# Row sums on one core: the seven rows that were loaded ahead of the whole groups go to the end

## The chip, the core and the metric

The kernel runs on one core of a Trainium2 chip. The metric is the time of one execution in microseconds (us). Before the change it is 161.35 us, the median of three runs (161.17, 161.35, 161.35).

The core's engines that matter here are SyncE (SP), which issues the loads and the last store; VectorE (DVE) and ScalarE (ACT), which add up rows; and 16 DMA engines, which move the data from the device memory (HBM) into the on-chip memory with its 128 partitions.

## The reference

The input `x` has 32 x 512 x 1024 float32 numbers, 67.1 MB. The output is the sum over the last axis, 32 x 512 numbers:

```python
return np.sum(x, axis=-1).astype(np.float32)
```

Each number is read once and added once, and the output is 64 KB.

## The kernel before

The 16,384 rows of 1024 numbers are spread over the 128 partitions, 128 rows to each. A group is 16 rows per partition (`BIG`): 16 x 1024 x 4 bytes are 64 KB per partition and 8.39 MB over all of them. There are eight groups. One, here called A, is the first 2048 rows of `x`, where a partition's 16 rows lie right behind those of the partition before (`x_a`). The other seven come from the rest (`x_b`), in which each partition has 112 rows in a row; they are called G (its rows 0 to 15) and B1 to B6 (rows 16 to 111). `rows_from` (L131) takes j below 112 as a place in `x_b`, and j from 112 on as one in `x_a`.

Each group needs an input buffer `t`, and there are three of them (L141), taken in turn. The order of the work is written out by hand; every engine follows the program's order, and the framework puts in the waits that the data needs. The steps before the change:

1. SP issues the first seven rows of G (L214, called F here) into the first buffer. A routine moves this very first load to the program's entry (L10). Its reduction on DVE is remembered as `first` (L215).
2. `wholes` (L216) lists A and then B1 to B6. The loop issues one load of 8.39 MB for each. A goes to the buffer `second`, of which DVE first fills four rows with zeros (L213); A's load therefore waits for that fill. B1's load (k == 1) is held until `first` is done (L223). From then on a load waits for the reduction that empties its buffer.
3. A and B1 to B5 are each summed by one DVE instruction of 128 x 16384 numbers (`vec`, L151). B6, the last, is summed row by row: nine rows on DVE, by an instruction that adds the two halves of a row and accumulates (`halves`, L164), and seven on ACT (`act`, L177).
4. The other nine rows of G follow in a fresh buffer (L227 to L237): a load of six rows (four on DVE, two on ACT), one of two rows (one and one), and the last row in two pieces of 560 and 464 numbers. DVE adds up the first piece into a cell behind the second, and the second with that cell.
5. Three stores put out the sums. Two, on ACT's queue, wait until the load of two rows has landed (L239, L240). The last, with the sums of G, goes from SP after the last DVE instruction (L243).

Of the kernel before, what the change touches and what calls it, by code (L numbers as in the profile page):

```python
# [100 lines left out]
@with_exitstack  # L101
def kernel(
    ctx: ExitStack,
    tc: tile.TileContext,
    x: bass.AP,
    out: bass.AP,
):
    nc = tc.nc
    nc.at_finalize(issue_first_load_at_entry)
    nc.at_finalize(order_waits)  # L110
    nc.at_finalize(wait_for_the_store_at_the_clear)
    fp32 = mybir.dt.float32
    P = 128
    batch, seq, dim = x.shape
    rows = batch * seq
    J = rows // P
    BIG = 16

    LONG = J - BIG
    rows_in = x.flatten_outer_dims()
    rows_out = out.rearrange("b s -> (b s)")
    x_a = rows_in[: P * BIG].rearrange("(p j) d -> p j d", p=P)
    x_b = rows_in[P * BIG :].rearrange("(p j) d -> p j d", p=P)
    out_a = rows_out[: P * BIG].rearrange("(p j) -> p j", p=P)
    out_b = rows_out[P * BIG :].rearrange("(p j) -> p j", p=P)


    def rows_from(j, n):  # L131
        return x_b[:, j : j + n, :] if j < LONG else x_a[:, j - LONG : j - LONG + n, :]

    last = 0
    FIRST = 7
    pieces = (560, 464)
    LINE = 64

    with (
        tc.tile_pool(name="small", bufs=1) as smallpool,  # L140
        tc.tile_pool(name="in", bufs=3) as inpool,  # L141
        tc.tile_pool(name="unread", bufs=4, space=bass.MemoryType.PSUM) as upool,
        tc.tile_pool(name="stage", bufs=1) as stpool,
        tc.manual_schedule(),
    ):


        seed = smallpool.tile([P, LINE // 2], fp32)
        sums = stpool.tile([P, J], fp32)

        def vec(dst, src):  # L151
            return nc.vector.tensor_reduce(  # L152
                out=dst, in_=src, axis=mybir.AxisListType.X, op=mybir.AluOpType.add
            )

        def hold(inst, until, reason):
            tc.add_manual_dep(
                inst.ins,
                until.ins.name,
                mybir.DependencyInfo(mybir.DependencyClass.Sync, mybir.DependencyReason.DATA),  # L160
                reason=reason,
            )

        def halves(dst, src):  # L164
            n = src.shape[-1] // 2
            return nc.vector.tensor_tensor_reduce(  # L166
                out=src[:, :n],
                in0=src[:, :n],
                in1=src[:, n:],
                scale=1.0,  # L170
                scalar=0.0,
                op0=mybir.AluOpType.add,
                op1=mybir.AluOpType.add,
                accum_out=dst,
            )

        def act(dst, src, n):  # L177
            unread = upool.tile([P, dim], fp32)
            nc.scalar.activation(  # L179
                out=unread[:, :n],  # L180
                in_=src,
                func=mybir.ActivationFunctionType.Copy,
                accum_out=dst,
            )

        sums_of = []

        def rows(t, a, n, j, n_act, pairs=False):
            nv = n - n_act
            block = t[:, a * dim : (a + n) * dim].rearrange("p (n d) -> p n d", d=dim)  # L190
            load = nc.sync.dma_start(out=block, in_=rows_from(j, n))  # L191
            if pairs:
                for q in range(nv):
                    sums_of.append(halves(sums[:, j + q : j + q + 1], block[:, q, :]))
            else:
                sums_of.append(vec(sums[:, j : j + nv], block[:, :nv, :]))
            for q in range(nv, n):
                act(sums[:, j + q : j + q + 1], block[:, q, :], dim)
            return load

        def store(eng, dst, j0, j1):
            return eng.dma_start(out=dst, in_=sums[:, j0:j1])

        nc.vector.memset(seed[:, :1], 0.0)  # L204
        unread = upool.tile([P, dim], fp32)
        ready = nc.scalar.activation(  # L206
            out=unread[:, :1], in_=seed[:, :1], func=mybir.ActivationFunctionType.Copy
        )

        j = last  # L210
        t = inpool.tile([P, BIG * dim + LINE], fp32)
        second = inpool.tile([P, BIG * dim + LINE], fp32, name="t")
        nc.vector.memset(second[:, : 4 * dim], 0.0)  # L213
        rows(t, 0, FIRST, j, 0)  # L214
        first = sums_of[-1]  # L215
        wholes = [LONG, *range(BIG, LONG, BIG)]  # L216
        for k, at in enumerate(wholes):
            t = second if k == 0 else inpool.tile([P, BIG * dim + LINE], fp32)
            if k < len(wholes) - 1:
                load = rows(t, 0, BIG, at, 0)  # L220
            else:
                rows(t, 0, BIG, at, 7, pairs=True)
            if k == 1:  # L223
                hold(load, first, "no descriptors of later loads while the first ones start")

        t = inpool.tile([P, BIG * dim + LINE], fp32)
        rows(t, FIRST, 6, j + FIRST, 2, pairs=True)  # L227
        two = rows(t, FIRST + 6, 2, j + FIRST + 6, 1, pairs=True)
        a = BIG - 1

        j += a
        c, width = pieces
        whole = t[:, a * dim + c : BIG * dim + 2]
        nc.vector.memset(whole[:, width + 1 :], 0.0)  # L234
        part = t[:, a * dim : a * dim + c]
        nc.sync.dma_start(out=part, in_=rows_from(j, 1)[:, 0, :c])  # L236
        nc.sync.dma_start(out=whole[:, :width], in_=rows_from(j, 1)[:, 0, c:])  # L237
        late = "its packets come behind those of the loads"
        hold(store(nc.scalar, out_b[:, BIG:], BIG, LONG), two, late)  # L239
        hold(store(nc.scalar, out_a, LONG, J), two, late)  # L240
        halves(whole[:, width : width + 1], part)
        halves(sums[:, j : j + 1], whole)
        store(nc.sync, out_b[:, :BIG], 0, BIG)  # L243
# [30 lines left out]
```

## Time and profile before

| what | value |
|---|---|
| median of three runs | 161.35 us |
| the profiled execution's own time | 161.16 us |
| its span in the trace | 159.4 us |
| time outside the span | 1.76 us |
| read from HBM | 67.11 MB, 421 GB/s over the span |
| DVE busy | 124.1 us (78%), 42 instructions |
| ACT busy | 12.1 us (8%), 22 instructions |
| share of the DMA queue with the loads | 97.9% of 16 engines' span |
| first load issued, first load landed | 0.00 us, 10.73 us |
| last DVE addition begins | 157.21 us |

Busy time is the time in which an engine executes; its share is of the span. A load "lands" when the engines that wait for it may go on. In a stretch of the trace, the GB/s times the length of the stretch gives the bytes of the DMA packets counted there; each packet here is one partition's part of one load.

### The profile page before, as it was taken

How to read it: one execution, taken by the hardware profiler on the slowest of the kernel's cores; microseconds unless marked ns; L12 is line 12 of the kernel's file. 1: busy time of each engine (PE TensorE's matmuls, PEld its weight loads, DVE VectorE, ACT ScalarE, POOL GpSimd, SP SyncE). 2: the span in 40 equal slices, each digit the busy share in tenths (PEclk: the TensorE clock that was granted, in tenths of full speed). 3: DMA queues.
4: the chain of work that ended last, by engine and by line, in shares of the span. 5: the costliest groups of instructions: out<-in, count | busy, mean ns of one | idle time of the engine just before them, and what ended most of it. 6: DMA issues, size and time to landing. Idle time of an engine off the chain costs nothing.

```text
span 159.4 us, 137 instructions
## 1 busy us (share of the span) xinstructions
DVE 124.1 (78%) x42; ACT 12.1 (8%) x22; POOL 0.2 (0%) x4
## 2 busy tenths in 40 slices
DVE  5339600499985999779995899949999499994955
ACT  3000000000000000000000000000000000003993
POOL 0000000000000000000000000000000000000000
DMA  9899999699699699699699797996996996995984
GB/s 324 374 486 526 395 395 526 280 510 526 263 526 526 263 526 526 263 526 526 263 526 461 329 526 313 477 526 263 526 526 263 526 526 263 526 526 247 444 371 139
DMA packets 2160, 67.18 MB, mean 421 GB/s; under 512 B 624, under 2 KB 752, under 8 KB 880
## 3 DMA queue, kind: packets, MB, share of 16 engines
q1 hardware_dynamic: 1872, 67.12, 97.9%
q10 hardware_dynamic: 288, 0.06, 0.2%
HBM read 67.11 MB, written 0.07 MB: 421 GB/s over the span
## 4 chain that ended last, share of the span: by engine, by line
DMA 71%; DVE 27%; SPq 1%; issue 0%; DVEq 0%
DMA t<-in_x_dram 71%; DVE sums L152 26%; SPq L191 0%; SPq L236 0%; DVE t L166 0%; DVEq L269 0%
## 5 line engine op out<-in xcount | busy, mean ns | idle before, releaser
L152 DVE TENSOR_REDUCE sums<-t 128x16 f32<-128x16384 f32 (+1 forms) x7 | 110.9, 15849 | 27.9 <-DMA t<-in_x_dram 27.9
L179 ACT ACTIVATE unread<-t 128x1024 f32<-128x1024 f32 x10 | 10.1, 1010 | 144.1 <-DMA t<-in_x_dram 144.1
L166 DVE CUSTOM_DVE_ANT_0 t<-t 128x512 f32<-128x512 f32 (+2 forms) x16 | 9.6, 656 | 4.0 <-DMA t<-in_x_dram 4.0
L213 DVE MEMSET t<- 128x4096 f32 x1 | 3.5, 3472 | 0.8 <-issue 0.8
L179 ACT ACTIVATION_READ_ACCUMULATOR unread<-t 128x1 f32 x10 | 1.9, 186 | 0.0
L206 ACT ACT_TABLE_LOAD x1 | 1.3, 1283 | 0.8 <-PEq L258 0.8
L166 DVE DVE_READ_ACCUMULATOR2_ANT sums<- 128x1 f32 x15 | 1.2, 83 | 0.0
L204 DVE MEMSET seed<- 128x1 f32 x1 | 0.1, 59 | 0.9 <-PEq L258 0.9
L206 ACT ACTIVATE unread<-seed 128x1 f32<-128x1 f32 x1 | 0.2, 174 | 0.0
L258 POOL MEMSET const-bfloat16-1.0<- 128x1 bf16 x1 | 0.1, 102 | 0.0
L258 POOL MEMSET const-uint8-127<- 128x1 uint8 x1 | 0.1, 102 | 0.0
L258 POOL MEMSET const-float32-0.0<- 128x1 f32 x1 | 0.1, 99 | 0.2 <-issue 0.2
L258 POOL MEMSET const-float32-1.0<- 128x1 f32 x1 | 0.1, 99 | 0.0
L166 DVE DVE_READ_ACCUMULATOR2_ANT t<- 128x1 f32 x1 | 0.1, 82 | 0.0
L234 DVE MEMSET t<- 128x1 f32 x1 | 0.1, 59 | 0.0
## 6 DMA issues: line engine op xcount, KB each, us to landing
t<-in_x_dram SPq DMA_DIRECT2D x1, 3584.0 KB, 10.7
t<-in_x_dram SPq DMA_DIRECT2D x1, 3072.0 KB, 28.7
t<-in_x_dram SPq DMA_DIRECT2D x1, 1024.0 KB, 30.8
t<-in_x_dram SPq DMA_DIRECT2D x1, 280.0 KB, 31.0
t<-in_x_dram SPq DMA_DIRECT2D x1, 232.0 KB, 31.1
t<-in_x_dram SPq DMA_DIRECT2D x7, 40.7
out_dram<-sums ACTq DMA_DIRECT2D x1, 48.0 KB, 1.6
out_dram<-sums ACTq DMA_DIRECT2D x1, 8.0 KB, 1.5
```

Source lines behind the costliest of these rows:

```text
L152: return nc.vector.tensor_reduce(out=dst, in_=src, axis=mybir.AxisListType.X, op=mybir.AluOpType.add)
L166: return nc.vector.tensor_tensor_reduce(out=src[:, :n], in0=src[:, :n], in1=src[:, n:], scale=1.0, scalar=0.0, op0=mybir.AluOpType.add, op ...
L179: nc.scalar.activation(out=unread[:, :n], in_=src, func=mybir.ActivationFunctionType.Copy, accum_out=dst,)
L204: nc.vector.memset(seed[:, :1], 0.0)
L206: ready = nc.scalar.activation(out=unread[:, :1], in_=seed[:, :1], func=mybir.ActivationFunctionType.Copy)
L213: nc.vector.memset(second[:, : 4 * dim], 0.0)
L234: nc.vector.memset(whole[:, width + 1 :], 0.0)
L258: nc = _bacc.Bacc("TRN2", target_bir_lowering=False, num_devices=1)
```

## The change

The loads that came first, seven rows of G, are gone from the front. A is now the first load, whole, into the first buffer, and the loop over `wholes` has the six groups B1 to B6 left, with B1 in the buffer `second`. `first`, for which the second load of the loop (now B2) is held, is a new ACT instruction that reads one number per partition of A's buffer, in place of the seven rows' DVE reduction. At the end G is loaded whole: nine rows (five on DVE, four on ACT), four rows (three and one), two rows (one and one), and the last row in the same two pieces as before.

```diff
     last = 0
-    FIRST = 7
+    NINE = 9
     pieces = (560, 464)
...
         nc.vector.memset(second[:, : 4 * dim], 0.0)
-        rows(t, 0, FIRST, j, 0)
-        first = sums_of[-1]
         wholes = [LONG, *range(BIG, LONG, BIG)]
+        rows(t, 0, BIG, wholes.pop(0), 0)
+        first = nc.scalar.activation(
+            out=unread[:, :1], in_=t[:, :1], func=mybir.ActivationFunctionType.Copy
+        )
         for k, at in enumerate(wholes):
             t = second if k == 0 else inpool.tile([P, BIG * dim + LINE], fp32)
...
         t = inpool.tile([P, BIG * dim + LINE], fp32)
-        rows(t, FIRST, 6, j + FIRST, 2, pairs=True)
-        two = rows(t, FIRST + 6, 2, j + FIRST + 6, 1, pairs=True)
+        rows(t, 0, NINE, j, 4, pairs=True)
+        rows(t, NINE, 4, j + NINE, 1, pairs=True)
+        two = rows(t, NINE + 4, 2, j + NINE + 4, 1, pairs=True)
         a = BIG - 1
```

## The prediction

> **What bounds the kernel now.** I read the page's totals first, then the chain that ended last, then the instructions in order of time, then short stretches of the start. F is the load of seven rows, A the contiguous group, B1 to B6 the other whole groups and G the group that is split.
>
> ```profile
> span 159.4 us, 137 instructions
> DVE 124.1 (78%) x42; ACT 12.1 (8%) x22; POOL 0.2 (0%) x4
> q1 hardware_dynamic: 1872, 67.12, 97.9%
> DMA 71%; DVE 27%; SPq 1%; issue 0%; DVEq 0%
> ```
>
> The queue with the loads fills 97.9% of the DMA engines' span. The chain's 27% on DVE looks like a second bound, but where a buffer's release lies on the chain the trace must say whether the queue was empty by then. The instructions in order of time settle that (start, duration, and in brackets the idle time before and what ended it):
>
> ```profile
> 1.74 3.47 DVE L213 MEMSET t<- 128x4096 f32 x1 [0.82 <-issue]
> 5.24 0.33 SPq L191 DMA_DIRECT2D t<-in_x_dram  x1
> 10.75 7.62 DVE L152 TENSOR_REDUCE sums<-t 128x7 f32<-128x7168 f32 x1 [5.54 <-DMA t<-in_x_dram]
> 18.40 0.81 SPq L191 DMA_DIRECT2D t<-in_x_dram  x2
> 30.17 17.22 DVE L152 TENSOR_REDUCE sums<-t 128x16 f32<-128x16384 f32 x1 [11.80 <-DMA t<-in_x_dram]
> 49.42 17.22 DVE L152 TENSOR_REDUCE sums<-t 128x16 f32<-128x16384 f32 x1 [2.03 <-DMA t<-in_x_dram]
> 124.70 0.81 SPq L191 DMA_DIRECT2D t<-in_x_dram  x2
> 126.80 17.22 DVE L152 TENSOR_REDUCE sums<-t 128x16 f32<-128x16384 f32 x1 [2.12 <-DMA t<-in_x_dram]
> 146.18 0.69 DVE L166 CUSTOM_DVE_ANT_0 t<-t 128x512 f32<-128x512 f32 x1 [2.16 <-DMA t<-in_x_dram]
> 155.86 1.03 ACT L179 ACTIVATE unread<-t 128x1024 f32<-128x1024 f32 x1 [0.22 <-DMA t<-in_x_dram]
> 156.57 0.45 DVE L166 CUSTOM_DVE_ANT_0 t<-t 128x280 f32<-128x280 f32 x1
> 157.21 0.40 DVE L166 CUSTOM_DVE_ANT_0 t<-t 128x233 f32<-128x233 f32 x1 [0.18 <-DMA t<-in_x_dram]
> ```
>
> The reader is to see that each DVE group begins when its load lands, after about 2.1 us of idling. A landed 30.17 - 10.75 = 19.42 after F, and from there to 146.18 six groups took (146.18 - 30.17) / 6 = 19.335 each, 433.9 GB/s. A reduction takes 17.22, so DVE frees a buffer 19.335 - 17.22 = 2.1 us ahead of the next landing, while one more whole load still waits in the queue: a margin of about 21 us. So the time is start + bytes / rate + tail. The start: F is 7/16 of a group, 8.46 us at that rate, and landed at 10.75, so 2.29 us come ahead. The tail: G's nine rows are 9/16, 10.88 us, and the last piece let DVE go 157.21 - 146.18 = 11.03 after B6, so 0.15 us are lost there; after it come 0.40 us of DVE, the store and the end.
>
> The start in short stretches (stretch and length, busy time of DVE, ACT and POOL, clock, DMA share, GB/s):
>
> ```profile
> 0.90:1.40 0.50, 0.02 (x1) 0.50 (x1) 0.00 (x0) 1.00 3.21 860
> 2.50:3.10 0.60, 0.60 (x1) 0.00 (x0) 0.00 (x0) 1.00 1.77 765
> 3.50:4.20 0.70, 0.70 (x1) 0.00 (x0) 0.00 (x0) 1.00 1.52 655
> 9.90:10.60 0.70, 0.00 (x0) 0.00 (x0) 0.00 (x0) 1.00 3.47 1498
> 14.70:15.40 0.70, 0.70 (x1) 0.00 (x0) 0.00 (x0) 1.00 3.46 1498
> ```
>
> 765 GB/s x 0.60 us are 459 KB, 16 packets of F (28 KB each); 1498 x 0.70 are 1.05 MB, 16 of A (64 KB each). A packet is thus counted as a whole where it begins, one per engine and round; the stretches left out between these hold none or one. F's rounds begin about 1.15 (15 packets), 2.80 and 3.85, and A's first at 10.25: seven steps of 1.064 after 2.80, but 1.65 for the first. So the first round costs 0.59 us extra, once. A's steps are (15.05 - 10.25) / 2 = 2.40.
>
> **The change, part by part.** The bytes are the same, and so is the number of loads by SP: ten plus two pieces, and 128 packets for each.
>
> The first load. A with 64 KB packets comes in place of F with 28 KB. The trace of before shows no whole load at a cold start. Taken as a fixed delay ahead of the first bytes, the 0.59 stays 0.59: cost 0. Upper bound, the delay as a share of the packet: 0.59 / 1.064 = 55% of 2.40 is 1.33, that is +0.74. Lower bound, no delay at all: -0.59. I take 0, since that late first round is one latency whatever follows, and keep both ends.
>
> The wait of the next loads. B1 takes A's place behind the zero fill, issued at 5.24; its first packets are due about 20.8, so 15 us of cover. B2 is held for the new ACT copy. A lands at 2.29 + 19.42 = 21.71; a copy of one number took 0.17 (L206), so B2 is issued by about 22 and is needed only when B1's transfer ends near 41: 19 us of cover. ACT has nothing else there. On SP, B3 to B6 and G stand behind B2, but each waits for a buffer that is freed later anyway. Cost 0; without cover it would be the delay beyond 41.
>
> The buffers. Landings: A 21.71, B1 41.05, and so on to B4 99.05, B5 118.4, B6 137.7. Three buffers in turn give B3 A's, B4 B1's, and G B4's. B3's load is issued at 21.71 + 17.26 = 38.97 and needed near 60. G's is freed at 99.05 + 17.25 = 116.30. SP issued the last four loads from 124.70 to 126.53; with one more at 0.4 it takes 116.3 to about 118.6, needed at 137. Cost 0.
>
> DVE and ACT. DVE loses the 7.62 us reduction and gets four more row pairs at 0.61 to 0.62 apart, 2.5 us; it begins 11 us later, but idles 2.1 us per group, and no backlog can arise while 17.22 is below 19.335. ACT gets three rows more at 1.04.
>
> The tail. G's 16 rows follow B6. Nine rows take 10.88: they land at 148.6; DVE's five pairs end about 151.8 and ACT's four rows at 152.8. Before that B6's own nine pairs and seven ACT rows (5.6 and 7.2 us in the trace) are done by 145. Four rows take 4.83: 153.4; three pairs end at 155.3, one ACT row at 154.6. Two rows: 155.85, as before. There DVE is now free 0.05 us earlier than before (its pair began at 155.91), but the last addition waits for the last piece, which had 0.18 us of idle ahead of it. It lands at 157.21 again. The seams between loads: six rows in the tail of before arrived within 0.02 of their share, F to A 0.085 above; I take 0 and keep -0.1 to +0.1. The stores wait for the same two rows. Cost 0.
>
> Sum: 2.29 + 19.42 + 6 x 19.335 + 10.88 + 0.15 + the unchanged end = the span of 159.4 again, and with the 1.76 outside it 161.16, this execution's own time. The median of the runs is 161.35, 0.19 above it; the four executions (161.16, 161.17, 161.35, 161.35) have their middle at 161.26. I predict 161.25.
>
> [...]
>
> **The rivals.**
>
> 1. *Slower: DVE's late start is not caught up.* DVE begins at 21.7, not 10.75, and has 7.62 - 2.5 = 5.1 us less to do, so if it were the bound the end moves by about 5.8 us: 167. It decides only if a reduction takes longer than a load, and every one of six idles before it. Chance 0.02.
>
> 2. *Slower: the cold first round grows with its packet.* This is the upper bound above: place, the first 4 us; price 0.74 at most; 161.99. It decides over 0.2% once more than half of it holds. For it: the first step is the only irregular one, and 16 engines begin at once with 2.3 times as many bytes. Against it: A's packets began in the same narrow step at 10.25 and ran at 2.40 with no loss. Chance 0.18.
>
> 3. *Faster: A starts better than F.* A's parts lie side by side in memory, F's are 448 KB apart. If more than a third of the 0.59 went, the time falls below 161.03; all of it gives 160.66. Against it: A's 19.42 is the longest step of all, so contiguity shows no advantage. Chance 0.12.
>
> 4. *A seam in the tail* (nine to four to two rows) leaves an engine behind the others: before, 0.15 was lost on the last nine rows; four times that gives 161.25 + 0.45 = 161.70, and just below that it decides. Chance 0.04.
>
> **How the numbers follow.** No effect has the remaining 0.64. About 0.2% (0.32 us) is what a measurement of this kernel tells from no change, so the band is 161.03 to 161.67. Slower is 0.02 + 0.18 + 0.04 = 0.24, faster 0.12. The range goes from 160.95, where the best of rival 3 is left out, to 162.1, which takes in all of rival 2 with 0.1 for the seams.
>
> **What the profile after would show.** The first whole reduction at 21.7, idle of about 2.1 before each later one, B6's pairs at 137.7, the two rows at 155.85, the last addition at 157.2. Rival 2 would shift all of these from the first on, with a first step of packets near 3.7 rather than 3.0; rival 3 would shift them the other way; rival 4 leaves B6 at 137.7 and moves the last addition. The prediction is wrong if A lands more than 0.3 us from 21.7 or if a load's landing interval leaves 19.3 to 19.4.

## The result and the profile after

The changed kernel takes 161.67 us (median of 12 runs, 161.50 to 161.78) where the kernel before, run beside it, takes 161.28 (12 runs). The ratio is 1.002, with a 95% interval of 1.0011 to 1.003: slower by 0.2%, or 0.39 us between the medians. I had predicted 161.25 and "no effect" as the likeliest case.

The profiled execution took 161.65 us. These lines of its page answer to those shown of before:

```profile
span 159.7 us, 153 instructions
DVE 119.1 (75%) x49; ACT 15.6 (10%) x29; POOL 0.2 (0%) x4
q1 hardware_dynamic: 1872, 67.12, 97.7%
```

The reader is to see three things. The loads' queue is as full as before (97.7% for 97.9%). DVE has less to do (119.1 us) but more instructions (49 for 42), because one reduction of seven rows became four row pairs of two instructions each. And the span is 159.7 us while the execution took 161.65: 1.95 us lie outside the span, where it was 1.76.

The instructions of the changed kernel in order of time (start, duration, idle time before and what ended it):

```profile
21.87 17.22 DVE L152 TENSOR_REDUCE sums<-t 128x16 f32<-128x16384 f32 x1 [16.67 <-DMA t<-in_x_dram]
41.25 17.22 DVE L152 TENSOR_REDUCE sums<-t 128x16 f32<-128x16384 f32 x1 [2.17 <-DMA t<-in_x_dram]
118.56 17.22 DVE L152 TENSOR_REDUCE sums<-t 128x16 f32<-128x16384 f32 x1 [2.10 <-DMA t<-in_x_dram]
137.92 0.69 DVE L166 CUSTOM_DVE_ANT_0 t<-t 128x512 f32<-128x512 f32 x1 [2.14 <-DMA t<-in_x_dram]
148.86 0.69 DVE L166 CUSTOM_DVE_ANT_0 t<-t 128x512 f32<-128x512 f32 x1 [5.34 <-DMA t<-in_x_dram]
153.72 0.69 DVE L166 CUSTOM_DVE_ANT_0 t<-t 128x512 f32<-128x512 f32 x1 [1.71 <-DMA t<-in_x_dram]
156.14 0.69 DVE L166 CUSTOM_DVE_ANT_0 t<-t 128x512 f32<-128x512 f32 x1 [0.49 <-DMA t<-in_x_dram]
157.48 0.40 DVE L166 CUSTOM_DVE_ANT_0 t<-t 128x233 f32<-128x233 f32 x1 [0.18 <-DMA t<-in_x_dram]
```

The order of events is the forecast one, and every wait shown is for a load. A landed at 21.87 (forecast 21.71), six groups later B6 at 137.92 (137.72), the nine rows at 148.86 (148.60), the two rows at 156.14 (155.85), and the last addition began at 157.48 (157.21). So 0.16 of the 0.27 us is there when the first load lands. From A to B6 it is 116.05 for 116.01, and from B6 to the last addition 19.56 for 8.46 + 11.03 = 19.49: another 0.07 at the end.

The start in short stretches, for the changed kernel (last column GB/s, the one before it the DMA share):

```profile
0.90:2.00 1.10, 0.28 (x2) 1.10 (x1) 0.00 (x0) 1.00 2.75 953
3.90:4.70 0.80, 0.80 (x1) 0.00 (x0) 0.00 (x0) 1.00 3.04 1311
6.30:7.00 0.70, 0.00 (x0) 0.00 (x0) 0.00 (x0) 1.00 3.46 1498
```

Each of these holds 1.05 MB, 16 packets of 64 KB, one per DMA engine. Before, A's packets of one round all began within 0.35 us of each other. Here a round takes 0.51 us to begin, by the packets' own times.

Each run lists its span beside its time, so the medians can be taken apart as well. Over 12 runs the changed kernel has 2.00 us outside its span. The kernel before has 1.78 outside, and spans of 159.44 to 159.53 in the means of its runs beside the experiments. The changed kernel's span is 159.66 in the mean. The 0.39 us is therefore about 0.22 outside the span and 0.13 to 0.22 inside it. The experiments take up these two parts.

### The profile page after: what moved, and what is told of

Read it like the earlier page. It is cut to its first block, busy times and chain, and to the rows that moved or that the text cites. A ratio compares the mean times of both kernels' runs of the same rounds, so it can differ in the third digit from the quotient of the medians.

```text
span 159.7 us, 153 instructions
## 1 busy us (share of the span) xinstructions
DVE 119.1 (75%) x49; ACT 15.6 (10%) x29; POOL 0.2 (0%) x4
## 3 DMA queue, kind: packets, MB, share of 16 engines
q1 hardware_dynamic: 1872, 67.12, 97.7%
## 4 chain that ended last, share of the span: by engine, by line
DMA 72%; DVE 24%; SPq 1%; issue 1%; DVEq 0%
DMA t<-in_x_dram 72%; DVE sums L152 22%; DVE t L213 2%; SPq L191 1%; SPq L239 0%; DVE t L166 0%; DVE seed L204 0%; DVEq L152 0%; DVEq L272 0%
## 5 line engine op out<-in xcount | busy, mean ns | idle before, releaser
L152 DVE TENSOR_REDUCE sums<-t 128x16 f32<-128x16384 f32 x6 | 103.3, 17220 | 27.3 <-DMA t<-in_x_dram 27.3
L179 ACT ACTIVATE unread<-t 128x1024 f32<-128x1024 f32 x13 | 13.2, 1013 | 121.3 <-DMA t<-in_x_dram 121.3
L166 DVE CUSTOM_DVE_ANT_0 t<-t 128x512 f32<-128x512 f32 (+2 forms) x20 | 12.2, 663 | 9.9 <-DMA t<-in_x_dram 9.9
L179 ACT ACTIVATION_READ_ACCUMULATOR unread<-t 128x1 f32 x13 | 2.4, 187 | 0.0
```

The lines of the kernel that those rows point to most:

```text
L152: return nc.vector.tensor_reduce(out=dst, in_=src, axis=mybir.AxisListType.X, op=mybir.AluOpType.add)
L166: return nc.vector.tensor_tensor_reduce(out=src[:, :n], in0=src[:, :n], in1=src[:, n:], scale=1.0, scalar=0.0, op0=mybir.AluOpType.add, op ...
L179: nc.scalar.activation(out=unread[:, :n], in_=src, func=mybir.ActivationFunctionType.Copy, accum_out=dst,)
```

## The experiments

The theories named in the expectations are these. Theory 1 comes from the prediction's second rival: with 64 KB packets the cold first round leaves the 16 DMA engines further apart, and the slowest stays behind. Theory 2 blames A's addresses at the cold start. Theory 3 blames the new end (nine, four and two rows). Theory 4 came from e1 to e4: the number of instructions sets the time outside the span. Times are medians; "outside" is the mean of a run's time less its span, with a standard error of 0.004 to 0.035.

### e1: A in two loads, seven rows and nine

```diff
-        nc.vector.memset(second[:, : 4 * dim], 0.0)
+        HEAD = 7
+        nc.vector.memset(t[:, HEAD * dim : HEAD * dim + 4 * dim], 0.0)
-        rows(t, 0, BIG, wholes.pop(0), 0)
+        at = wholes.pop(0)
+        for a, n in ((0, HEAD), (HEAD, BIG - HEAD)):
+            nc.sync.dma_start(
+                out=t[:, a * dim : (a + n) * dim].rearrange("p (n d) -> p n d", d=dim),
+                in_=rows_from(at + a, n),
+            )
+        vec(sums[:, at : at + BIG], t[:, : BIG * dim].rearrange("p (n d) -> p n d", d=dim))
```

(Against the changed kernel; the ACT copy reads the last number of the buffer instead of the first.)

> The changed kernel, but A is loaded in two parts, seven rows (28 KB packets) and, behind the zero fill, nine rows; one reduction still takes all 16. Theory 1 (cold start: with 64 KB packets the 16 DMA engines leave the first round further apart, and the slowest stays behind to the end): as the kernel before, 161.2 to 161.45 us, A landing near 21.7. Theory 2 (A's addresses, 64 KB from partition to partition, are what a cold start does badly): 161.6 to 161.7, A landing near 21.85. Theory 3 (the new end, nine, four and two rows, costs it): 161.6 to 161.75.

Measured: 161.87 us, ratio to the kernel before 1.0042 (1.0029 to 1.0054), 2.09 outside. A landed at 22.09 in the profile, which is of the slowest of its five executions (162.22). Theory 1 in its plain form fails: small first packets brought nothing back, and the run is even 0.2 us slower than the changed kernel. A second seam and two issues at 5.24 came with the edit, so it does not price the packet size by itself.

### e2: B1 first, A second

```diff
-        wholes = [LONG, *range(BIG, LONG, BIG)]
+        wholes = [BIG, LONG, *range(2 * BIG, LONG, BIG)]
```

(Against the changed kernel.)

> The changed kernel with A and B1 exchanged: the first whole load is B1, with its parts 448 KB apart; A comes second. Theory 1 (size of the first packets): as the changed kernel, 161.6 to 161.75, first landing 21.85 or later. Theory 2 (A's addresses at the cold start): 161.2 to 161.4, first landing near 21.7. Theory 3 (the end): 161.6 to 161.75, but with the first landing anywhere.

Measured: 161.85 us, ratio 1.003 (1.0015 to 1.0045), 2.12 outside, mean span 159.72; the first load landed at 22.10. Theory 2 fails as the cause: with A out of the first place the time is no better. It is 0.1 us above the range of theory 1 too.

### e3: the seven rows from A

```diff
-    last = 0
+    last = LONG
...
-        wholes = [LONG, *range(BIG, LONG, BIG)]
+        wholes = [0, *range(BIG, LONG, BIG)]
...
-        hold(store(nc.scalar, out_a, LONG, J), two, late)
+        hold(store(nc.scalar, out_b[:, :BIG], 0, BIG), two, late)
...
-        store(nc.sync, out_b[:, :BIG], 0, BIG)
+        store(nc.sync, out_a, LONG, J)
```

(Against the kernel before.)

> The kernel before with the parts of A and G exchanged: the first seven rows come from A, its other nine at the end, and G is loaded whole in A's place. Theory 1: as the kernel before, 161.2 to 161.4, the seven rows landing at 10.7 to 10.8. Theory 2: slower, 161.45 to 161.7, the seven rows landing 0.15 or more after 10.75. Theory 3: as the kernel before.

Measured: 161.40 us, ratio 1.0008 (0.9999 to 1.0017), 1.80 outside, mean span 159.59 beside 159.53 of the kernel before. The seven rows landed at 11.09 in the one profile, which fits theory 2 (G's seven rows landed at 10.75 to 10.94 in six profiles). The median falls on the edge between theories 1 and 2: A's addresses cost some 0.06 us in the span, near the limit of what can be told.

### e4: one seam more near the end

```diff
-        rows(t, FIRST, 6, j + FIRST, 2, pairs=True)
+        rows(t, FIRST, 3, j + FIRST, 1, pairs=True)
+        rows(t, FIRST + 3, 3, j + FIRST + 3, 1, pairs=True)
```

(Against the kernel before.)

> The kernel before with its load of six rows near the end cut into two of three (two on DVE and one on ACT each): one more load, its packets smaller. Theory 3 (a seam near the end costs 0.08 to 0.1 each): 161.35 to 161.5. Theories 1 and 2: no more than 0.05 from the kernel before.

Measured: 161.31 us, ratio 1.0003 (0.9994 to 1.0011), 1.77 outside. A seam here costs nothing that these runs can tell, and neither does one load more on SP.

These four show a division that none of the first three theories makes: e1, e2 and the changed kernel have 2.00 to 2.12 us outside the span, e3, e4 and the kernel before 1.77 to 1.80. The first set has 49 DVE and 29 ACT instructions in the trace, the second 42 and 22. That is theory 4.

### e5 and e6: the kernel before with idle instructions, on DVE or on ACT

e5 adds, behind `first = sums_of[-1]`:

```diff
+        for k in range(8):
+            nc.vector.memset(seed[:, 4 + k : 5 + k], 0.0)
```

e6 adds at the same place of the program:

```diff
+        for k in range(4):
+            nc.scalar.activation(
+                out=unread[:, :1],
+                in_=seed[:, :1],
+                func=mybir.ActivationFunctionType.Copy,
+                accum_out=seed[:, 4 + k : 5 + k],
+            )
```

> The kernel before with eight more DVE instructions, each a zero fill of one number per partition, behind the seven rows' reduction, where DVE idles for 11.8 us. Theory 4 (the time outside the span, 1.78 us for the kernel before and 2.00 for the changed one, grows with the number of instructions, on DVE): 161.4 to 161.55, the span as before, 0.15 to 0.25 more outside it. Theory 4 with ACT as the engine that counts, and theory 1: 161.2 to 161.35.

> The kernel before with four more ACT additions of one number per partition (eight ACT instructions in the trace), at the start, where ACT idles. Theory 4 with ACT as the engine that counts: 161.4 to 161.55, 0.15 to 0.25 more outside the span. Theory 4 with DVE, and theory 1: 161.2 to 161.35.

The pages of e5 and of e6:

```profile
span 159.5 us, 145 instructions
DVE 124.2 (78%) x50; ACT 12.1 (8%) x22; POOL 0.2 (0%) x4
```

```profile
span 159.5 us, 145 instructions
DVE 124.1 (78%) x42; ACT 13.3 (8%) x30; POOL 0.2 (0%) x4
```

Measured: e5 161.55 us, ratio 1.0021 (1.0012 to 1.003), 2.06 outside; e6 161.22, ratio 1.0001 (0.9992 to 1.001), 1.80 outside. The pages show the same span and the same number of instructions; only the engine differs. Eight zero fills of some 0.06 us each, in a stretch where DVE idles for 11.8 us, cost 0.3 us of time without a trace in the span. Eight ACT instructions cost nothing.

### e7 and e8: the changed kernel with fewer instructions

e7, against the changed kernel:

```diff
-                rows(t, 0, BIG, at, 7, pairs=True)
+                rows(t, 0, BIG, at, 7)
```

e8 has `rows(t, 0, BIG, at, 4)` there, so that DVE reduces twelve rows of B6 in one instruction and ACT adds four.

> The changed kernel, with B6's nine DVE rows summed by one reduction (about 9.7 us, done before the next landing) in place of nine pairs: 17 DVE instructions fewer, ACT as in the changed kernel. Theory 4 on DVE: the time outside the span falls from 2.00 to 1.8 or less, 161.2 to 161.45. Theory 4 on ACT, and theory 1: 161.6 to 161.75.

> The changed kernel, with twelve of B6's rows summed by one DVE reduction (about 12.9 us; the pairs of the nine rows begin 2 us late and are done before the four rows' last pair is due) and four by ACT: DVE 17 and ACT 6 instructions fewer. Theory 4 on either engine: 161.2 to 161.45. Theory 1 alone: 161.6 to 161.75. A late DVE at the end would show as a last addition beyond 157.5.

The lines of e7's profile that show the edit, the page's first and then B6's reduction:

```profile
span 159.6 us, 135 instructions
DVE 123.3 (77%) x32; ACT 15.6 (10%) x29; POOL 0.2 (0%) x4
```

```profile
137.89 9.76 DVE L152 TENSOR_REDUCE sums<-t 128x9 f32<-128x9216 f32 x1 [2.15 <-DMA t<-in_x_dram]
```

Measured: e7 161.43 us, ratio 1.0015 (1.0007 to 1.0024), e8 161.42, ratio 1.0012 (1.0003 to 1.0021); 1.78 outside in both. With DVE at 32 instructions the 0.22 us outside are gone, though ACT still has 29 in e7. What remains inside the span remains: 159.69 and 159.67 beside 159.44 of the kernel before. Going below 42 instructions gains nothing further, so the time outside is no price per instruction.

### e11 and e12: 4 and 24 DVE instructions more than before

The edit of e5, with `range(4)` and `range(24)`.

> The kernel before with four more DVE instructions (46 in all, where eight more, 50, gave 2.06 us outside the span). If the time outside grows with each instruction beyond 42: about 1.92 us outside, 161.35 to 161.4. If it is one step: either 1.78 (161.2 to 161.3) or 2.0 to 2.06 (161.45 to 161.6).

> The kernel before with 24 more DVE instructions (66 in all), done in DVE's idle time. If the time outside grows with each instruction: 2.6 us outside or more, 162.0 and up. If it is one step between 42 and 50: 2.0 to 2.1 us outside, 161.45 to 161.65.

Measured: e11 161.62 us, ratio 1.0026 (1.0017 to 1.0036), 2.21 outside, the span unchanged (159.48 beside 159.48): a step, though higher than the 2.06 of eight instructions. e12 161.85, ratio 1.0038 (1.0025 to 1.0051), 1.77 outside, but a mean span of 160.08. Neither expectation holds for e12: the cost is neither per instruction nor one step outside the span. It has moved into the span, and the page of e12 has a third queue there (DMA queue, kind: packets, MB, share):

```profile
q1 hardware_dynamic: 1872, 67.12, 97.5%
q10 hardware_dynamic: 288, 0.06, 0.2%
q14 instruction: 1, 0.01, 0.0%
```

The end of e12 in order of time, and then the line of the kernel before for the landing of the same six rows:

```profile
146.20 0.69 DVE L166 CUSTOM_DVE_ANT_0 t<-t 128x512 f32<-128x512 f32 x1 [2.10 <-DMA t<-in_x_dram]
154.21 1.03 ACT L179 ACTIVATE unread<-t 128x1024 f32<-128x1024 f32 x1 [0.63 <-DMA t<-in_x_dram]
154.21 0.69 DVE L166 CUSTOM_DVE_ANT_0 t<-t 128x512 f32<-128x512 f32 x1 [2.42 <-DMA t<-in_x_dram]
157.90 0.40 DVE L166 CUSTOM_DVE_ANT_0 t<-t 128x233 f32<-128x233 f32 x1
```

```profile
153.45 0.69 DVE L166 CUSTOM_DVE_ANT_0 t<-t 128x512 f32<-128x512 f32 x1 [1.67 <-DMA t<-in_x_dram]
```

The third queue of e12's page, with one packet of instructions, is on no page shown so far. The trace records packets beyond the span too. There five to seven 8 KB packets of that kind precede the kernel in each run, and in some one more comes late:

```
kernel      DVE instructions   outside us  late instruction packet, 8192 bytes, us after the first instruction
e7 to e10, e14            32  1.77 - 1.80  none
before, e3, e4, e6        42  1.77 - 1.80  none
e13                       44         2.05  none recorded
e11                       46         2.21  none recorded
after                     49         2.00  161.50
e1, e2                    49   2.09, 2.12  161.94, 161.69
e5                        50         2.06  161.29
e12                       66         1.77  152.83 (inside the span)
```

So the late packet goes with DVE's count in these profiles: none with 32 or 42 instructions, one behind the last store with 49 and 50 (161.29 to 161.94 us; in the changed kernel the last store's packets begin by 158.96), one inside the span with 66. What sets its time is not shown, and the records do not say for which engine it is; that DVE's count matters and ACT's does not is shown by e5 and e6 (2.06 us outside with eight more on DVE, 1.80 with eight more on ACT). There are four profiles with a packet behind the end. The packet's own time differs (0.38, 0.51, 0.49 and 0.54 us in after, e1, e2 and e5), yet in each of them it ends 0.23 us beyond the execution's own time, counted from the first instruction (161.88 for 161.65, 162.45 for 162.22, 162.18 for 161.95, 161.83 for 161.60). That the end of the execution waits for the packet is my estimate from these four pairs of numbers.

With 66 instructions the packet comes at 152.83, while the last rows are loading: the six rows land 154.21 - 146.20 = 8.01 us after B6 instead of 153.45 - 146.18 = 7.27. ACT, which also waits for them, begins at 154.21 too, so the load is late, and not DVE alone. By the times of the 16 signals that this load is there, 15 DMA engines were through by 153.47 and the last at 154.19 (before, all 16 by 153.43). A packet of the next load, which begins where the instruction packet ends (153.14), took 0.83 us, where the others took 0.31. Everything behind is late: DVE reaches the last addition at 157.90 without any idle time ahead of it, as the last of e12's lines shows. For 44 and 46 instructions no late packet is recorded though the time outside is as long or longer (2.05 and 2.21 us); why is open, and that a packet plays a part in these two runs is not shown.

### e9 and e10: smaller first packets in one load

Both build on e7. A's rows are laid out in 2 or 8 blocks with gaps between them, so that one load is cut into packets of 32 or 8 KB:

```diff
-        rows(t, 0, BIG, wholes.pop(0), 0)
+        CUTS = 2
+        each = BIG // CUTS
+        at = wholes.pop(0)
+        spaced = t[:, :].rearrange("p (b w) -> p b w", b=CUTS)[:, :, : each * dim]
+        nc.sync.dma_start(
+            out=spaced, in_=rows_from(at, BIG).rearrange("p (b n) d -> p b (n d)", b=CUTS)
+        )
+        vec(
+            sums[:, at : at + BIG].rearrange("p (b n) -> p b n", b=CUTS),
+            spaced.rearrange("p b (n d) -> p b n d", d=dim),
+        )
```

> The kernel with nine rows of B6 in one reduction (so 1.78 us outside the span), with A's rows laid out with a gap of 32 numbers between the halves of the buffer: the same first load in packets of 32 KB instead of 64 KB. Theory 1 (what is left inside the span, about 0.2 us, comes from 64 KB packets at the cold start): span 159.45 to 159.6, 161.2 to 161.35. Theory 3 (it comes from the end, where nine, four and two rows take 0.07 more, and from other places): span 159.65 to 159.75, 161.4 to 161.5.

> The same with A's rows in eight blocks of two: first packets of 8 KB. Theory 1: as with 32 KB or lower, span 159.35 to 159.55, 161.1 to 161.3. Theory 3: span 159.65 to 159.75, 161.4 to 161.5; more packets may add up to 0.1.

The first load's issue in e9 and in e7:

```profile
0.00 0.65 SPq L219 DMA_DIRECT2D t<-in_x_dram  x1
```

```profile
0.00 0.36 SPq L191 DMA_DIRECT2D t<-in_x_dram  x1
```

Measured: e9 161.92 us, ratio 1.0043 (1.0029 to 1.0058), span 160.14; e10 162.05, ratio 1.0052 (1.0038 to 1.0066), span 160.32. Both are far from either expectation. The load cut into blocks takes SP 0.65 us to issue instead of 0.36, and its first packets begin at 1.42 us where e7's begin at 0.99. So the edit delays the start by 0.43 us and does not test the size alone. What it does show is that finer first packets, got in this way, cost more than they could bring: A landed 0.53 us later than in e7 with two blocks and 1.03 us later with eight, more than the 0.43 to 0.45 us of the delayed start.

### e13: four rows ahead instead of seven

```diff
-    FIRST = 7
+    FIRST = 4
...
-        rows(t, FIRST, 6, j + FIRST, 2, pairs=True)
-        two = rows(t, FIRST + 6, 2, j + FIRST + 6, 1, pairs=True)
+        rows(t, FIRST, 6, j + FIRST, 3, pairs=True)
+        rows(t, FIRST + 6, 3, j + FIRST + 6, 1, pairs=True)
+        two = rows(t, FIRST + 9, 2, j + FIRST + 9, 1, pairs=True)
```

(Against the kernel before.)

> The kernel before with four rows ahead instead of seven (first packets of 16 KB), and G's other twelve at the end as six, three and two rows and the last in its pieces: 44 DVE instructions in the trace and one load more. If the spread of the 16 DMA engines in the first round grows with the packet: a span of 159.3 to 159.5, below or at that of the kernel before in spite of the extra load. If it does not: 159.45 to 159.65. The time outside the span: 1.78 if 44 instructions still fit in what was fetched ahead, 2.0 to 2.2 if not.

The profile of e13 in order of time:

```profile
7.58 4.42 DVE L152 TENSOR_REDUCE sums<-t 128x4 f32<-128x4096 f32 x1 [2.39 <-DMA t<-in_x_dram]
28.05 17.22 DVE L152 TENSOR_REDUCE sums<-t 128x16 f32<-128x16384 f32 x1 [16.05 <-DMA t<-in_x_dram]
```

Measured: 162.12 us, ratio 1.0063 (1.0047 to 1.0078), span 160.20, 2.05 outside. The profile is of the slowest of the six executions (162.95 us). In it A landed 20.47 us after the four rows instead of 19.42. Its load was issued at 5.24, and the first DMA engine was through with the four rows at 6.5. One engine began A's first packet only at 7.65, and the other 15 took 2.5 to 2.9 us for theirs, against 2.42 before. The engines were 1.5 us apart from then on. That A's load was issued too late for such a short first load is my reading; no run moves the issue alone. This loss hides what a smaller first packet does, so the size stays untested here too. The run does put the step in the time outside the span between 42 and 44 instructions (1.78 and 2.05 us). Whether 44 instructions "still fit in what was fetched ahead" is not shown by that, since no late instruction packet is recorded here.

### e14: the end cut as before

```diff
-    NINE = 9
+    SEVEN = 7
...
-        rows(t, 0, NINE, j, 4, pairs=True)
-        rows(t, NINE, 4, j + NINE, 1, pairs=True)
-        two = rows(t, NINE + 4, 2, j + NINE + 4, 1, pairs=True)
+        rows(t, 0, SEVEN, j, 3, pairs=True)
+        rows(t, SEVEN, 6, j + SEVEN, 2, pairs=True)
+        two = rows(t, SEVEN + 6, 2, j + SEVEN + 6, 1, pairs=True)
```

(Against e7.)

> The kernel with nine rows of B6 in one reduction (1.78 us outside the span, span 159.69), with G at the end as seven, six and two rows instead of nine, four and two: the last nine rows are loaded as in the kernel before. If the 0.07 us that the end takes more come from the cut into nine and four: span 159.6 to 159.65, and 19.49 from B6's landing to the last addition. If they come from engines that are further apart from the first round on: span 159.65 to 159.75, and 19.55 to 19.57.

```profile
137.96 9.75 DVE L152 TENSOR_REDUCE sums<-t 128x9 f32<-128x9216 f32 x1 [2.18 <-DMA t<-in_x_dram]
157.51 0.40 DVE L166 CUSTOM_DVE_ANT_0 t<-t 128x233 f32<-128x233 f32 x1 [0.17 <-DMA t<-in_x_dram]
```

Measured: 161.42 us, ratio 1.0011 (1.0002 to 1.0019), mean span 159.63, 1.79 outside. From B6 to the last addition it is 19.55 us, as with nine, four and two rows. Theory 3 falls: the cut of the last group does not make the 0.07.

### What the traces say together about the start

For each profile but those of e9, e10 and e13, which start in other ways, one can take how far the 16 engines are apart in a round (first to last packet begun, at 45 us, in the middle of a whole load), and how long after the start the second load's bytes are complete, less those bytes at 433.9 GB/s:

```
first load                       apart, us                          ahead of the bytes, us
G's seven rows (before, e4, e5,  0.33 0.56 0.46 0.47 0.27 0.34       2.38 2.53 2.52 2.56 2.36 2.46
  e6, e11, e12)
A's seven rows (e1, e3)          0.59 0.60                           2.66 2.67
whole A (after, e7, e8, e14)     0.53 0.55 0.72 0.45                 2.58 2.58 2.75 2.59
whole B1 (e2)                    0.68                                2.80
```

Engines that begin apart stay apart: 0.51 us in the changed kernel's second round, 0.52 at 25 us, 0.57 at 96 us. A load lands when the slowest engine is through: the 16 signals of A in the changed kernel come from 21.33 to 21.84 us, and the reduction begins at 21.87. With G's seven rows first the mean loss is 2.47 us, with a whole load 2.66. Those 0.19 us in single profiles, and 0.07 at the end, agree in size with the 0.13 to 0.25 us by which the spans of whole-first kernels exceed that of the kernel before. Single profiles carry some chance, though: the distances of the first and the third row overlap (0.56 in e4, 0.45 in e14), and e3 has 2.66 in its profile while the spans of its 11 runs are only 0.06 us longer.

The means over the 16 engines tell more of the first round. From its beginning to that of the second round it takes 3.02 us in the changed kernel, 0.60 more than the later rounds of 2.42, and 1.67 us before, 0.61 more than the later 1.06. Over the profiles of the first row of the table the surplus is 0.54 to 0.67 us, over the last two rows 0.56 to 0.69. So the mean delay did not grow with the packet. What grew is how far the last engine is behind the mean in the second round: 0.30 us in the changed kernel (4.57 for 4.27) against 0.15 before (2.98 for 2.83), and 0.25 to 0.46 against 0.12 to 0.31 over the same profiles.

Whether the size of the first packets, their addresses or both set the spread is open. B1 whole, with the same distance between partitions as G's seven rows, speaks for the size; A's seven rows speak for the addresses. The finer packets of e9 and e10 did not bring the engines together (0.65 and 0.86 us apart at 45 us), though their start differs in other ways too.

No kernel here beats the kernel before; e3, e4 and e6 equal it within their intervals.

## Why the prediction was wrong

- *The sum's last step*, "and with the 1.76 outside it 161.16", failed. I carried the time outside the span over as a constant. It rose to 2.00 us with seven more DVE instructions; that the end waited for the instruction packet recorded at 161.50 us is my estimate. e5 puts that price on the kernel before, and e7 and e8 take it off the changed one. I had counted the four more row pairs at 2.5 us of hidden DVE work, which they are; as instructions they were not hidden. This is the larger part, 0.22 of 0.39 us.
- *The cold start*, "I take 0, since that late first round is one latency whatever follows", was mis-sized. A landed at 21.87, 0.16 later than the sum says, within the bounds kept (-0.59 to +0.74). Rival 2 had the place right, and its sign: the term is 0.1 to 0.2 and not 0.74. Its mechanism, a delay that grows with the packet, did not come: the mean delay of the first round stayed (0.60 us for 0.61), and the first step was 3.0 and not 3.7. My picture was incomplete, since I took the round's mean step, and a load lands with the slowest of 16 engines, which came 0.15 us further behind the mean. Whether the packet's size causes that is not shown.
- *The tail*, cost 0, was 0.07 us too low, in every profile with a whole load first that shows the last addition (19.53 to 19.56 us after B6). In the changed kernel's profile 0.06 of it is there when the nine rows land (10.94 us after B6 for 10.88). Neither the cut nor a seam is the reason (e14, e4). Rival 4 was therefore wrong in its mechanism; the cause is open.
- *The waits, the buffers and DVE's late start* cost nothing, as said: B2's load was issued at 22.07 and needed near 41, G's loads left SP from 116.49 to 118.82, and DVE idled 2.0 to 2.2 us ahead of each of the six later groups. Rival 1 did not come into play.
- *Rival 3* (A starts better) was wrong in sign: A landed later, and e3's rows of A did not come sooner.
- *The range* held 161.67, but by luck: its upper part was drawn for rival 2, its working put the 0.64 on no effect, and no case in it had the time outside the span change. The 0.2% taken as the least that a measurement can tell was too coarse as well: with 12 runs on each side the interval begins at 1.0011.
- *A small slip*, which moves nothing: loads landed 19.26 to 19.40 us apart after and 19.25 to 19.42 before, so that the sign "leaves 19.3 to 19.4" was too narrow from the start.

## What to carry to other kernels

A trade of one long instruction for several short ones can have a price in instructions as well as in busy time: here seven more on DVE went with 2.00 us outside the span instead of 1.78, and 24 more with an instruction packet among the last loads and a span of 160.08 us instead of 159.48. So compare the time outside the span too. In this kernel, which is all loads, the DMA engines stayed as far apart as the first round left them for most of the run (0.51 us in the second round after the change, 0.57 at 96 us), and a load landed with the slowest of them. In the kernel before, the second load was issued at 5.24 us, 4.8 us before the first DMA engine began on it, and followed without a loss; in e13 it was issued 1.3 us before the first engine was through with the four rows, and landed 20.47 us after them instead of 19.42 (one profile).

## What the runs showed of the hardware that I had not expected

- A packet of 8 KB in the instruction queue behind the end went with 0.22 to 0.34 us more outside the span (after, e1, e2, e5: 49 and 50 DVE instructions), and in all four profiles it ended 0.23 us beyond the execution's own time. With 44 and 46 it was 0.27 and 0.43 us more, but no such packet is recorded. Inside the span, beside the loads of the last rows, one went with some 0.6 us of span (e12: 160.08 for 159.48). One DMA engine's 8 KB packet of a load took 0.83 us there, where the others took 0.31.
- The distance between the 16 DMA engines, 0.27 to 0.72 us after the cold starts with packets of 28 or 64 KB, changes by only about 0.1 us over some 130 us of loads in the two profiles of before and after (from 0.35 us at 2.6 us to 0.29 at 143, and from 0.51 at 4.1 to 0.62 at 137).
- A load in two blocks per partition took SP 0.65 us to issue instead of 0.36, and its first packet began 0.43 us later (e9 beside e7).
